# Gate groups and operand sums of a hybrid decoder layer placed ahead of, and inside, the branch products

## The chip, the cores and the metric

One core of one Trainium2 chip runs the whole layer in one launch. The metric is the device time of one execution in microseconds (us), the median of several runs. Engines are named as in the profile: PE is the matrix engine (PEld its weight loads), DVE the vector engine, ACT the scalar engine, POOL the GpSimd engine and SP the engine that issues most transfers.

## What is computed

A decoder layer on 512 tokens of width 2048, float32 in and out. The part that matters here, shortened from the reference:

```
hq, hf, hi, hg, aq, ak, av, ga, gb = split(x @ w_in)
y_a = hgrn2_mixer(hq, hf, hi, hg, ...) @ w_branch_a
y_b = swa_sink_attention(rope(aq), rope(ak), av, sinks) @ w_branch_b
mixed = sigmoid(ga) * y_a + sigmoid(gb) * y_b
x = layer_norm(ALPHA * x + mixed @ w_out, ...)
h = square(relu(x @ w_ff1)) @ w_ff2
x = layer_norm(ALPHA * x + h, ...)
```

## The kernel before

All matrix products run on PE in float32r. Each factor is split by `split` (L82) into a high half, a copy made by ACT (L84), and a low half, a subtraction made by DVE (L85). `mm3` (L113) then issues three matmuls, on L114 (high, high), L115 and L116 (one low half each). Weights arrive in blocks of 128x1024: a transfer on SP, then the two halves `wh` and `wl`.

The stages follow one another: the projections with the attention, the HGRN2 recurrence over eight heads in four pairs (`hg_pair`, L519), the branch products (L687), the gates (L712 on), the output projection with the first layer norm, and the feed-forward part.

- **Tail of the recurrence.** The last pair ends with `hg_out` (L479) once for each head: PE makes the state updates (L483), DVE chains them (L486, L488), PE makes the outputs (L493, L495), ACT squares them (L499), DVE does a dozen small steps for the root (L152 to L158) and a product (L502), PE transposes (L506), and DVE writes the head into `oT` (L508). Each step waits for the one before.
- **Branch products.** `att` (the attention's output) and `oT` (the recurrence's) are split into `half` tiles, eight slices of 128x512 each. Then eight groups of 256 columns for `wb` and eight for `wa` follow, 48 matmuls of 512 columns in a group, made by `proj_fm` (L118) with two weight blocks. ACT copies each result out of PSUM (L695), POOL stores it to `yd` (L696).
- **Gates.** `NPLAIN = 2` groups (one of gate B, one of gate A) are made the plain way, 96 matmuls of 512 columns each (`plain`, L552). The other fourteen use `Sevens` (L635), which makes seven products of half width instead of eight. It needs seven operands of the activation: four are quarters of `bh`/`bl` (one of them, q5, overwritten), three (`xq`: q3, q6, q7) are new. `operands` (L595) makes them with sums on DVE (`tt`, L590) in a scratch tile `room`, then splits them. `merge` (L701) loads `yd` into `room`, takes the sigmoid, multiplies, and stores or adds the product to `md`.

Tiles come from rings by tag: `mz` (four buffers: `att`, `oT`, later the pairs `raws` of `pair`), `h` (four: `half` tiles, `xq` tiles, `room`), `r` (two: results), `mm` (four PSUM banks). The pool of `h` and `r` lies over the memory of the recurrence, which is closed first (L541). The builder lays out one list of instructions for each engine, and each engine works its list in that order.

Of the kernel before, what the change touches and what calls it, by code (L numbers as in the profile page):

```python
# [17 lines left out]
P = 128  # L18
# [34 lines left out]
def layer(ctx, tc, xt, xn, win, wg, wa, wb, wo1, wo2, w1, w2, cst, vec, lnv, out):  # L53
# [512 lines left out]
    def flat(r):  # L566
        return r[:].rearrange("p n t -> p (n t)")
# [24 lines left out]
    def wide():  # L592
        return pf.tile([P, 4, 1024], F32, tag="h", bufs=4, name=nm("room"))

    def operands(room):  # L595

        xo = {"q1": (bh[:, 0:8, 0:CG], bl[:, 0:8, 0:CG]), "q2": (bh[:, 8:16, 0:CG], bl[:, 8:16, 0:CG]),
              "q5": (bh[:, 0:8, CG:T], bl[:, 0:8, CG:T]), "q4": (bh[:, 8:16, CG:T], bl[:, 8:16, CG:T])}
        for q in ("q6", "q7", "q3"):
            t_ = pf.tile([P, 2, 8, CG], F32R, tag="h", bufs=4, name=nm("x" + q))  # L600
            xo[q] = (t_[:, 0], t_[:, 1])
        for u in range(2):
            k = slice(4 * u, 4 * u + 4)
            r0, r1, r2, r3 = (room[:, i, :].rearrange("p (k c) -> p k c", k=4) for i in range(4))

            def whole(r, q):
                tt(r, xo[q][0][:, k, :].bitcast(F32), xo[q][1][:, k, :].bitcast(F32), ALU.add)

            def put(q, src):
                split(xo[q][0][:, k, :], xo[q][1][:, k, :], src)  # L610

            whole(r0, "q1")
            whole(r1, "q5")
            tt(r2, r0, r1, ALU.subtract)
            put("q7", r2)
            whole(r3, "q4")
            tt(r3, r1, r3, ALU.add)
            tt(r0, r3, r0, ALU.subtract)
            put("q6", r0)
            whole(r1, "q2")  # L620
            tt(r1, r1, r0, ALU.subtract)
            put("q3", r1)
            put("q5", r3)
        return xo

    def tmp(tag, bufs):
# [51 lines left out]
            self.left = (g, B, C, U2, E, t2_, b22, R)  # L678


    yd = [[pd.tile([P, 1024], F32, name=f"yd{i}_{c}") for c in range(8)] for i in range(2)]
    md = [pd.tile([P, 1024], F32, name=f"md{c}") for c in range(8)]

    def half():
        return pf.tile([P, 8, T], F32R, tag="h", bufs=4, name=nm("half"))

    for i, (w, y) in enumerate(((wb, att), (wa, oT))):  # L687
        yh, yl = half(), half()
        for k in range(8):
            split(yh[:, k, :], yl[:, k, :], y[k // 4][:, k % 4, :])  # L690
        for c in range(8):
            o = proj_fm([w[c, q] for q in range(2)], yh, yl)
            r = result()
            for m in range(2):
                ACT.activation(r[:, m, :], o[m][:], AF.Copy)  # L695
            nc.gpsimd.dma_start(out=yd[i][c][:], in_=flat(r))  # L696


    room = wide()

    def merge(g, R):  # L701

        y = room[:, 2 + g % 2, :]
        nc.scalar.dma_start(out=y, in_=yd[g % 2][g // 2][:])
        ACT.activation(R[:], R[:], AF.Sigmoid)
        tt(flat(R), flat(R), y, ALU.mult)
        if g % 2:
            nc.gpsimd.dma_start(out=md[g // 2][:], in_=flat(R), accum_op=ALU.add)
        else:
            nc.gpsimd.dma_start(out=md[g // 2][:], in_=flat(R))  # L710

    NPLAIN = 2  # L712
    for g in range(NPLAIN):
        o = [ps("mm"), ps("mm")]
        plain(wg[g], o, None)
        R = result()
        for m in range(2):
            ACT.activation(R[:, m, :], o[m][:], AF.Copy)
        if g == NPLAIN - 1:
            xo = operands(room)  # L720
        merge(g, R)
    sevens = Sevens(xo, room, merge)
    for g in range(NPLAIN, 16):
        sevens.group(g, wg[g])
# [125 lines left out]
            ACT.activation(r[:, m, :], og[g][m][:], AF.Relu)  # L850
        keep(g, r)
    room = wide()
    sevens = Sevens(operands(room), room, relu)
    for g in range(NHEAD, NG):
        sevens.group(g, w1[g])
    sevens.rest()
# [168 lines left out]
```

## Time and profile before

| | |
|---|---|
| median of 3 runs | 2714.32 us (2712.2 to 2715.52) |
| the profiled execution | 2713.84 us |
| its span on the core | 2712.1 us |
| busy: PE, DVE, ACT, POOL | 98%, 60%, 43%, 6% |
| mean granted clock of PE | 0.991 of full speed |

The span is what the trace covers; 1.74 us of the execution's time lie around it. PE's busy share counts matmuls whose ends are modelled and overlap, so 98% says that PE is nearly always at work, not how fast. The granted clock says how much of full speed (2.4 GHz) the throttle let through; 0.5 is 1.2 GHz. In rows of the timeline the columns are start, duration, engine, line, operation, output and inputs, shapes, the count, and in brackets the idle time before it and what ended that.

### The profile page before, as it was taken

Reading aid. Unit: us, or ns where it says so; the run is one execution under the profiler, and the core shown is the slowest. Engines: PE = TensorE matmul, PEld = TensorE weight load, DVE = VectorE, ACT = ScalarE, POOL = GpSimd, SP = SyncE. Lnnn points to the kernel's source line nnn. Section 1 sums busy time; section 2 is a strip of 40 time slices with the busy share of each in tenths; the row PEclk is TensorE's granted clock in tenths of the full one; section 3 lists DMA queues with packets and bytes.
Section 4 is the critical chain, followed back from the end, with each engine's and each line's share of the span. In section 5 each row is a group of like instructions: output and inputs, shape, how many; then the busy total and the mean of one; then the engine's idle time right before and its main releaser. Section 6 shows DMA issues by size and latency. Waiting matters only on the chain.

```text
span 2712.1 us, 39517 instructions
## 1 busy us (share of the span) xinstructions
PE 2652.9 (98%) x16272; PEld 2382.2 (88%) x16272; DVE 1637.7 (60%) x2121; ACT 1168.3 (43%) x1597; POOL 169.3 (6%) x168
## 2 busy tenths in 40 slices
PE   8999999998998999999999999999999999999997
PEld 7889788986887999988989999999998888888886
DVE  4588785664226878733768777777754444433346
ACT  4576655353233444421444444444444333322231
POOL 0110322210000000000200000000000000000001
PEclk9999999998998999999999999999999999999999
DMA  5222212223443455652452333333366555434442
GB/s 186 89 75 78 76 58 85 77 78 140 155 140 93 141 156 164 205 175 94 172 194 102 133 133 125 133 137 122 131 236 236 187 198 190 171 141 153 151 176 78
DMA packets 104437, 377.27 MB, mean 139 GB/s; under 512 B 11712, under 2 KB 12480, under 8 KB 102720
## 3 DMA queue, kind: packets, MB, share of 16 engines
q1 hardware_dynamic: 88128, 313.91, 33.3%
q0 software_dynamic: 10368, 41.95, 4.5%
q10 hardware_dynamic: 5760, 18.88, 2.2%
q8 instruction: 128, 2.10, 0.3%
q14 instruction: 53, 0.43, 0.0%
HBM read 332.75 MB, written 41.94 MB: 138 GB/s over the span
## 4 chain that ended last, share of the span: by engine, by line
PE 92%; DVE 5%; ACT 1%; DMA 1%; issue 1%; POOL 0%; DVEq 0%; SPq 0%; ACTq 0%
PE mm L114 21%; PE mm L116 21%; PE mm L115 21%; PE tp L116 7%; PE tp L114 7%; PE tp L115 7%; PE sc L115 1%; PE sc L114 1%; PE sc L116 1%; DVE wl L85 1%; PE tp L444 1%; DVE room L590 1%; DMA raw<-w 1%; PE tp L285 0%; PE tp L277 0%
## 5 line engine op out<-in xcount | busy, mean ns | idle before, releaser
L114 PE MATMUL mm<-bh,wh 128*128 128x256 f32 (+1 forms) x1808 | 585.6, 324 | 3.9 <-ACT wh L84 2.4
L116 PE MATMUL mm<-bh,wl 128*128 128x256 f32 (+1 forms) x1808 | 585.0, 324 | 0.5 <-DVE wl L85 0.4
L115 PE MATMUL mm<-bl,wh 128*128 128x256 f32 (+1 forms) x1808 | 585.4, 324 | 0.0
L84 ACT ACTIVATE wh<-raws 128x1024 fp32r<-128x1024 f32 x332 | 350.2, 1056 | 493.0 <-PE mm L115 319.6
L85 DVE TENSOR_TENSOR wl<-raws,wh 128x1024 fp32r<-128x1024 f32 x332 | 404.8, 1223 | 239.0 <-ACT wh L84 238.4
L85 DVE TENSOR_TENSOR wl<-raw,wh 128x1024 fp32r<-128x1024 f32 (+1 forms) x183 | 221.4, 1210 | 343.3 <-PE mm L116 193.2
L114 PEld LDWEIGHTS mm<-bh,wh 128*128 128x128 f32 x1808 | 344.9, 191 | 30.7 <-ACT wh L84 3.2
L116 PEld LDWEIGHTS mm<-bh,wl 128*128 128x128 f32 x1808 | 344.7, 191 | 26.5 <-DVE wl L85 0.9
L115 PEld LDWEIGHTS mm<-bl,wh 128*128 128x128 f32 x1808 | 344.9, 191 | 25.4
L84 ACT ACTIVATE wh<-raw 128x1024 fp32r<-128x1024 f32 (+1 forms) x183 | 190.9, 1044 | 303.9 <-PE mm L115 153.4
L85 DVE TENSOR_TENSOR hl<-raws,hh 128x1024 fp32r<-128x1024 f32 x94 | 114.8, 1224 | 235.3 <-ACT hh L84 235.1
L84 ACT ACTIVATE hh<-raws 128x1024 fp32r<-128x1024 f32 x94 | 99.1, 1058 | 264.3 <-PE mm L115 252.9
L114 PE MATMUL mm<-xq,wh 128*128 128x256 f32 x672 | 191.6, 285 | 10.8 <-ACT wh L84 10.2
L116 PE MATMUL mm<-xq,wl 128*128 128x256 f32 x672 | 191.3, 285 | 1.5 <-DVE wl L85 1.4
L115 PE MATMUL mm<-xq,wh 128*128 128x256 f32 x672 | 191.1, 284 | 0.0
L115 PE MATMUL mm<-wl,hh 128*128 128x512 f32 x472 | 183.6, 389 | 0.0
L114 PE MATMUL mm<-wh,hh 128*128 128x512 f32 x472 | 183.6, 389 | 0.0
L116 PE MATMUL mm<-wh,hl 128*128 128x512 f32 x472 | 183.6, 389 | 0.0
L114 PE MATMUL mm<-wh,bh 128*128 128x256 f32 (+1 forms) x448 | 139.2, 313 | 7.6 <-ACT bh L84 6.0
L114 PEld LDWEIGHTS mm<-xq,wh 128*128 128x128 f32 x672 | 130.1, 194 | 11.2 <-ACT wh L84 10.4
L115 PE MATMUL mm<-wl,bh 128*128 128x256 f32 (+1 forms) x448 | 138.8, 311 | 0.8 <-DVE wl L85 0.8
L114 PE MATMUL tp<-wh,hh 128*128 128x512 f32 x356 | 138.5, 389 | 0.0
(318 smaller groups left out, 5494.3 us busy)
## 6 DMA issues: line engine op xcount, KB each, us to landing
raws<-w SPq DMA_DIRECT2D x240, 512.0 KB, 4.5
raws<-hd SPq DMA_DIRECT2D x96, 512.0 KB, 3.8
raw<-win SPq DMA_DIRECT2D x87, 512.0 KB, 3.2
raws<-wg SPq DMA_DIRECT2D x56, 512.0 KB, 4.1
raw<-wo SPq DMA_DIRECT2D x32, 512.0 KB, 3.3
hd<-r POOLq DMA_DIRECT2D x32, 512.0 KB, 2.9
raw<-w SPq DMA_DIRECT2D x24, 512.0 KB, 3.6
raw<-wb SPq DMA_DIRECT2D x16, 512.0 KB, 3.6
```

The source lines that it names most:

```text
L84: ACT.activation(hi, src, AF.Copy)
L85: DVE.tensor_tensor(lo, src, hi.bitcast(F32), op=ALU.subtract)
L114: PE.matmul(o, ah, bh_, start=first, stop=False, skip_group_check=True)
L115: PE.matmul(o, ah, bl_, start=False, stop=False, skip_group_check=True)
L116: PE.matmul(o, al, bh_, start=False, stop=last, skip_group_check=True)
L444: PE.matmul(pl[:, c * P:(c + 1) * P], qk[:, c * P:(c + 1) * P], qk[:, c * P:(c + 1) * P], start=True, stop=True)
L590: DVE.tensor_tensor(dst, a, b, op=op)
```

## The change

Two plain groups of gates move ahead of the branch products, with the sigmoid in their evictions, and are stored to a new buffer `gd`. The first group of each branch (c = 0) is merged at once: `gd` is loaded into a second result tile, multiplied on DVE, and stored or added to `md`. The other seven groups of a branch go to `yd` as before. `operands` now stands after the branch products in the code, with its scratch in four `mz` pairs in place of `room`, with q7 allocated ahead of q6, and with q5 put ahead of the q2 and q3 steps. `Sevens` starts at group 2 as before. The feed-forward part calls the same `operands` with slices of `room`.

```diff
--- before.py
+++ after.py
@@ -592,16 +592,17 @@
     def wide():
         return pf.tile([P, 4, 1024], F32, tag="h", bufs=4, name=nm("room"))
 
-    def operands(room):
+    def operands(rooms):
+
 
         xo = {"q1": (bh[:, 0:8, 0:CG], bl[:, 0:8, 0:CG]), "q2": (bh[:, 8:16, 0:CG], bl[:, 8:16, 0:CG]),
               "q5": (bh[:, 0:8, CG:T], bl[:, 0:8, CG:T]), "q4": (bh[:, 8:16, CG:T], bl[:, 8:16, CG:T])}
-        for q in ("q6", "q7", "q3"):
+        for q in ("q7", "q6", "q3"):
             t_ = pf.tile([P, 2, 8, CG], F32R, tag="h", bufs=4, name=nm("x" + q))
             xo[q] = (t_[:, 0], t_[:, 1])
         for u in range(2):
             k = slice(4 * u, 4 * u + 4)
-            r0, r1, r2, r3 = (room[:, i, :].rearrange("p (k c) -> p k c", k=4) for i in range(4))
+            r0, r1, r2, r3 = (r.rearrange("p (k c) -> p k c", k=4) for r in rooms(u))
 
             def whole(r, q):
                 tt(r, xo[q][0][:, k, :].bitcast(F32), xo[q][1][:, k, :].bitcast(F32), ALU.add)
@@ -617,10 +618,10 @@
             tt(r3, r1, r3, ALU.add)
             tt(r0, r3, r0, ALU.subtract)
             put("q6", r0)
+            put("q5", r3)
             whole(r1, "q2")
             tt(r1, r1, r0, ALU.subtract)
             put("q3", r1)
-            put("q5", r3)
         return xo
 
     def tmp(tag, bufs):
@@ -678,8 +679,24 @@
             self.left = (g, B, C, U2, E, t2_, b22, R)
 
 
+    gd = [pd.tile([P, 1024], F32, name=f"gd{i}") for i in range(2)]
     yd = [[pd.tile([P, 1024], F32, name=f"yd{i}_{c}") for c in range(8)] for i in range(2)]
     md = [pd.tile([P, 1024], F32, name=f"md{c}") for c in range(8)]
+
+    def add_md(c, i, r):
+        if i:
+            nc.gpsimd.dma_start(out=md[c][:], in_=r, accum_op=ALU.add)
+        else:
+            nc.gpsimd.dma_start(out=md[c][:], in_=r)
+
+    for i in range(2):
+        o = [ps("mm"), ps("mm")]
+        plain(wg[i], o, None)
+        r = result()
+        for m in range(2):
+            ACT.activation(r[:, m, :], o[m][:], AF.Sigmoid)
+        nc.gpsimd.dma_start(out=gd[i][:], in_=flat(r))
+
 
     def half():
         return pf.tile([P, 8, T], F32R, tag="h", bufs=4, name=nm("half"))
@@ -693,9 +710,19 @@
             r = result()
             for m in range(2):
                 ACT.activation(r[:, m, :], o[m][:], AF.Copy)
-            nc.gpsimd.dma_start(out=yd[i][c][:], in_=flat(r))
-
-
+            if c:
+                nc.gpsimd.dma_start(out=yd[i][c][:], in_=flat(r))
+            else:
+                gt = result()
+                nc.sync.dma_start(out=flat(gt), in_=gd[i][:])
+                tt(flat(r), flat(r), flat(gt), ALU.mult)
+                add_md(0, i, flat(r))
+
+
+    def rooms(u):
+        return [x for _ in range(2) for x in (lambda t: (t[:, 0, :], t[:, 1, :]))(pair())]
+
+    xo = operands(rooms)
     room = wide()
 
     def merge(g, R):
@@ -704,21 +731,9 @@
         nc.scalar.dma_start(out=y, in_=yd[g % 2][g // 2][:])
         ACT.activation(R[:], R[:], AF.Sigmoid)
         tt(flat(R), flat(R), y, ALU.mult)
-        if g % 2:
-            nc.gpsimd.dma_start(out=md[g // 2][:], in_=flat(R), accum_op=ALU.add)
-        else:
-            nc.gpsimd.dma_start(out=md[g // 2][:], in_=flat(R))
+        add_md(g // 2, g % 2, flat(R))
 
     NPLAIN = 2
-    for g in range(NPLAIN):
-        o = [ps("mm"), ps("mm")]
-        plain(wg[g], o, None)
-        R = result()
-        for m in range(2):
-            ACT.activation(R[:, m, :], o[m][:], AF.Copy)
-        if g == NPLAIN - 1:
-            xo = operands(room)
-        merge(g, R)
     sevens = Sevens(xo, room, merge)
     for g in range(NPLAIN, 16):
         sevens.group(g, wg[g])
@@ -850,7 +865,7 @@
             ACT.activation(r[:, m, :], og[g][m][:], AF.Relu)
         keep(g, r)
     room = wide()
-    sevens = Sevens(operands(room), room, relu)
+    sevens = Sevens(operands(lambda u: [room[:, i, :] for i in range(4)]), room, relu)
     for g in range(NHEAD, NG):
         sevens.group(g, w1[g])
     sevens.rest()
```

How the lists of instructions move, at three places. First PE, from the last projection of the recurrence (`mm_5588`) into the two `hg_out` of the last pair; before:

```order
L116 MATMUL mm_5588<-wh_5752,bl 128x256
L483 MATMUL sc_5808<-v_5805,kT_5461 128x128 x3
L493 MATMUL sc_5816<-v_5805,SB_2016 128x128 x2
L495 MATMUL sc_5816<-state_5812,qe_5450 128x128
L493 MATMUL sc_5816<-v_5805,SB_2016 128x128
L495 MATMUL sc_5816<-state_5812,qe_5450 128x128
L493 MATMUL sc_5816<-v_5805,SB_2016 128x128
L495 MATMUL sc_5816<-state_5812,qe_5450 128x128
L506 MATMUL sc_5847<-ident,on_5825 128x128 x4
L483 MATMUL sc_5853<-v_5805,kT_5585 128x128 x3
```

Now the matmuls of the plain groups (`mm_5929` is the first PSUM bank of the first one) stand around these steps:

```order
L116 MATMUL mm_5929<-bh,wl_5933 128x512
L114 MATMUL mm_5929<-bh,wh_5932 128x512
L483 MATMUL sc_5808<-v_5805,kT_5461 128x128 x3
L115 MATMUL mm_5929<-bl,wh_5932 128x512
L116 MATMUL mm_5929<-bh,wl_5933 128x512
```

Of the 192 plain matmuls, 19 now stand ahead of the first L483, 25 between it and L493, 45 from there to L506, 23 to the second L483, 25 to L493, 46 to the second L506, and nine after it; then the first branch group begins. Before, none stood between these steps.

Second, ACT where the branch products begin; before:

```order
L499 ACTIVATE on_5825,ss_5824<-sc_5816 128x128 x4
L499 ACTIVATE on_5870,ss_5869<-sc_5861 128x128 x4
L84 ACTIVATE half_5927<-att_522 128x512 x4
L84 ACTIVATE half_5927<-att_523 128x512 x4
L84 ACTIVATE half_6473<-oT_2020 128x512 x4
```

and now:

```order
L499 ACTIVATE on_5870,ss_5869<-sc_5861 128x128 x4
L84 ACTIVATE wh_6202<-raw_6201 128x1024
L84 ACTIVATE wh_6232<-raw_6231 128x1024
L697 ACT_TABLE_LOAD
L697 ACTIVATE r_6051<-mm_5929 128x512
L697 ACTIVATE r_6051<-mm_5930 128x512
L697 ACTIVATE r_6177<-mm_6055 128x512
L84 ACTIVATE half_6181<-att_522 128x512 x4
L84 ACTIVATE half_6181<-att_523 128x512 x4
```

The evictions of the plain groups (L697, with a table load) now stand between the last squares of the recurrence and the first `half`. On DVE in the same stretch the sums of `operands` (L590 on `raws`) now stand between the halves and the `wl` of the first four branch groups:

```order
L590 TENSOR_TENSOR raws_7282<-bh,bl 128x1024 x2
L85 TENSOR_TENSOR half_6182<-att_523,half_6181 128x512
L85 TENSOR_TENSOR half_6731<-oT_2020,half_6730 128x512 x3
L85 TENSOR_TENSOR wl_6272<-raw_6270,wh_6271 128x1024
L85 TENSOR_TENSOR half_6731<-oT_2020,half_6730 128x512
L85 TENSOR_TENSOR half_6731<-oT_2021,half_6730 128x512 x2
L590 TENSOR_TENSOR raws_7283<-raws_7282 128x1024
L590 TENSOR_TENSOR raws_7283<-bh,bl 128x1024
L85 TENSOR_TENSOR half_6731<-oT_2021,half_6730 128x512 x2
L590 TENSOR_TENSOR raws_7300<-bh,bl 128x1024 x2
L85 TENSOR_TENSOR wl_6302<-raw_6300,wh_6301 128x1024
L590 TENSOR_TENSOR r_6261<-r_6261,r_6264 128x1024
```

`wl_6272` and `wl_6302` belong to the second branch group, and row L590 on `r_6261` is the product of the first merged group. In the list of before this stretch has the 16 halves and then nothing but `wl`.

Third, ACT where `Sevens` begins, behind the last branch product (`mm_7213`, `mm_7214`; `wh_7363` is the first split out of `room`):

```order
L712 ACTIVATE r_7275<-mm_7213 128x512
L84 ACTIVATE xq_1123_7281<-raws_7282 128x1024
L84 ACTIVATE xq_1123_7281<-raws_7300 128x1024
L712 ACTIVATE r_7275<-mm_7214 128x512
L731 DMA room_7318<-yd_1_5906 128x1024
L731 DMA room_7318<-yd_1_5914 128x1024
L84 ACTIVATE wh_7363<-room_7318 128x1024
L84 ACTIVATE wh_7392<-raws_7326 128x1024
```

Before, at the same place, ACT's list had the evictions, sigmoids and operand splits of the plain groups:

```order
L718 ACTIVATE r_7271<-mm_7149 128x512
L718 ACTIVATE r_7271<-mm_7150 128x512
L705 ACTIVATE r_7271<-r_7271 128x1024
L84 ACTIVATE xq_1121_7275<-room_7019 128x1024
L660 ACTIVATE E_7317<-mm_7313 128x256
L84 ACTIVATE bh<-room_7019 128x4x256
L84 ACTIVATE xq_1120_7274<-room_7019 128x1024
L704 DMA room_7019<-yd_1_5904 128x1024
L704 DMA room_7019<-yd_0_5911 128x1024
L84 ACTIVATE xq_1122_7276<-room_7019 128x1024
L84 ACTIVATE wh_7357<-room_7019 128x1024
```

Only the splits of q3 (`xq_1123`) are left there; those of q7, q6 and q5 moved up into the branch products. But for a few rows in the first two groups of `Sevens`, all lists are the same as before from there on.

## Rows read from the trace of the kernel before

**Rows 1.** The page, busy time, share of the span, instructions of each engine
```profile
PE 2652.9 (98%) x16272; PEld 2382.2 (88%) x16272; DVE 1637.7 (60%) x2121; ACT 1168.3 (43%) x1597; POOL 169.3 (6%) x168
```

**Rows 2.** Waits of PE, whole span: who waited for whom, us, times, longest
```profile
PE mm L114 <- ACT wh L84: 14.2, 6, 10.2
PE sc L506 <- DVE on L502: 8.9, 2, 4.4
```

**Rows 3.** Windows: stretch, length, busy PE PEld DVE ACT POOL, PEclk, DMA share, GB/s
```profile
612.26:641.26 29.00, 16.18 (x63) 13.01 (x64) 16.09 (x48) 10.54 (x31) 0.00 (x0) 0.65 0.14 49
858.74:876.70 17.96, 6.17 (x26) 5.59 (x26) 17.10 (x15) 7.38 (x9) 0.90 (x1) 0.62 0.51 127
641.26:855.84 214.58, 214.58 (x949) 177.77 (x948) 70.10 (x63) 65.72 (x83) 9.32 (x17) 1.00 0.43 146
```

**Rows 4.** Timeline of the recurrence's tail, ACT and PE
```profile
616.03 0.39 PE L495 MATMUL sc<-state,qe 128*128 128x128 f32 x2
...
620.85 1.09 PE L506 MATMUL sc<-ident,on 128*128 128x128 f32 x4 [4.43 <-DVE on L502]
...
634.54 4.27 ACT L84 ACTIVATE half<-att 128x512 fp32r<-128x512 f32 x8 [4.43 <-PE sc L506]
```

**Rows 5.** Timeline of an earlier head, matmuls of the same kind at full clock
```profile
348.39 0.39 PE L495 MATMUL sc<-state,qe 128*128 128x128 f32 x2
348.61 0.39 PE L493 MATMUL sc<-v,SB 128*128 128x128 f32 x2
```

**Rows 6.** Timeline of PE where `Sevens` starts
```profile
858.34 0.28 PE L115 MATMUL mm<-bl,wh 128*128 128x256 f32 x1
858.46 0.28 PE L116 MATMUL mm<-bh,wl 128*128 128x256 f32 x1
868.98 0.58 PE L114 MATMUL mm<-xq,wh 128*128 128x256 f32 x1 [10.24 <-ACT wh L84]
...
872.12 0.58 PE L116 MATMUL mm<-xq,wl 128*128 128x256 f32 x1 [1.40 <-DVE wl L85]
```

**Rows 7.** Tile `half` and line L705: count, duration ns min/median/max, first and last start
```profile
L84 ACT ACTIVATE half<-att x8: 610/612/629, 634.5 to 638.2; 128x512 fp32r<-128x512 f32 x8
L85 DVE TENSOR_TENSOR half<-att,half x8: 684/685/691, 635.2 to 639.4; 128x512 fp32r<-128x512 f32 x8
...
L705 ACT ACTIVATE r<-r x16: 1042/1044/1062, 836.8 to 1160.8; 128x1024 f32<-128x1024 f32 x16
L705 ACT ACT_TABLE_LOAD  x1: 1283/1283/1283, 835.5 to 835.5; - x1
```

**Rows 8.** Timeline of DVE and ACT around the operands: steps of 128x1024 operations
```profile
846.05 1.22 DVE L85 TENSOR_TENSOR xq<-room,xq 128x1024 fp32r<-128x1024 f32 x1
847.19 1.22 DVE L85 TENSOR_TENSOR bl<-room,bh 128x1024 fp32r<-128x1024 f32 x1
...
863.20 1.46 ACTq L704 DMA_DIRECT2D room<-yd  x2
...
868.83 1.99 ACT L84 ACTIVATE wh<-raws 128x1024 fp32r<-128x1024 f32 x2
```

**Rows 9.** Short idle times of PE elsewhere, and windows of 2 us behind the second
```profile
347.84 0.71 PE L493 MATMUL sc<-v,SB 128*128 128x128 f32 x4 [1.71 <-DVE state L488]
1345.82 0.63 PE L792 MATMUL tp<-ident,z 128*128 128x128 f32 x4 [1.33 <-DVE z L783]
...
1347.00:1349.00 2.00, 1.58 (x9) 1.47 (x8) 2.00 (x3) 2.00 (x4) 0.60 (x2) 0.66 0.30 59
1349.00:1351.00 2.00, 2.00 (x11) 2.00 (x11) 2.00 (x4) 2.00 (x4) 2.00 (x2) 0.50 0.98 350
```

**Rows 10.** Tiles `yd`, `md`, `room`, in order: transfers from issue to landing, min/median/max
```profile
DMA to landing us min/median/max: 2.9/4.7/7.2
DMA to landing us min/median/max: 2.9/5.4/9.4
DMA to landing us min/median/max: 3.3/4.0/6.1
```

## Prediction

> **What bounds the kernel now.** The page comes first: PE is busy for 98% of the span and no other engine for more than 60% [rows 1]. So time is saved only where PE idles or runs at half clock. The second view, the waits of PE, says where: the longest single wait is 10.2 us for ACT's weight halves, and DVE's product `on` (L502) costs 8.9 us in two pieces [rows 2]. The third view, windows over the stretches around these waits, gives their price with the clock in it [rows 3]. In the first, 612.26 to 641.26 us, the granted clock is 0.65; in the second, 858.74 to 876.70, it is 0.62. Between them lie 214.58 us with 949 matmuls of 512 columns, at full clock and without a gap: 0.226 us for one.
>
> *First gap, the tail of the recurrence.* The window has 63 matmul rows. Fifteen are of the first branch group: 15 x 0.226 = 3.4 us. The other 48 belong to the last two heads. At full clock two such rows start 0.22 us apart [rows 5], 0.11 for one, so they are 5.3 us of work. Of 29.0 us, 20.3 are lost. The timeline shows how: PE ends L495 at about 616.4, and idles 4.43 us until DVE delivers `on` at 620.85; from there it runs at half clock [rows 4].
>
> *Second gap, the start of `Sevens`.* The window has 26 matmuls of 256 columns, which start 0.12 us apart at full clock [rows 6]: 3.1 us of work in 17.96, so 14.8 lost. PE waits 10.24 us for ACT's split of `room` and 1.40 more for DVE's [rows 6], while DVE works without a pause (17.10 of 17.96 us, [rows 3]) on the operand sums, which could not be finished beside the two plain groups.
>
> Together 35.1 us are lost. PE's work is the same before and after, so the forecast is these 35.1 us less what the new order loses in its own places.
>
> **The change, part by part.** *Plain groups into the tail.* 192 matmuls x 0.226 = 43.4 us of PE work now stand between the steps of the two heads. By the list, 45 of them (10.2 us) separate L495 from the first L506, and 46 the second. The chain that they cover took 4.8 us (616.03 to 620.85, [rows 4]); two `wl` halves that DVE now makes ahead of it add 2 x 1.14 us (the step of such operations, [rows 8]), and one of them waits up to 0.9 us for the end of a weight block. That is 8.0 us against 10.2. The shorter steps have 23 to 25 matmuls, over 5 us, for under 3 us of DVE work. Nothing here should be waited for: 20.3 us come back, and the first branch group starts at full clock.
>
> *Start of the branch products.* `half` lies over memory of the recurrence, so ACT begins only when the second L506 has ended, as before [rows 4]. New in front of it are a table load and three evictions. The load is 1.28 us [rows 7]; an eviction has the shape of a `half` copy, which start 0.6 us apart or less [rows 7]. With the first copy: 1.28 + 3 x 0.6 + 0.61 = 3.7 us. The transposes end some 0.25 us after PE goes on, and the nine plain matmuls behind them cover 2.0. PE waits 3.7 + 0.25 - 2.0 = 2.0 us. The low half then takes DVE 0.69 us [rows 7], of which two matmuls cover 0.45: 0.3 more. Cost 2.3 us. The trace has sixteen sigmoids with copies among them and one load [rows 7], after which the next operation starts at once; so one load is charged and no second one for the copies behind. The Trainium skill ("ScalarE: Activation LUTs", What ACT_TABLE_LOAD costs) speaks against this place: it puts a drain of about 1.38 us beside the 1.28 us of each switch. By an estimate from that page the wait here would be 3.7 us and not 2.3, and the sum 1.4 us worse.
>
> *Operand sums into the branch products.* The sums, 16 operations, and six of the eight low halves of 128x1024 leave the second gap; the two of q3 stay at the start of `Sevens`. By the list most of the sums stand on DVE among the halves and `wl` of the first four branch groups. From the first low half to the second `wl` of branch group two, DVE has 16 halves x 0.6, six sums and two `wl` x 1.14: 18.7 us. PE passes 78 matmuls, 17.6 us, from 0.75 us later: it waits 0.4. To the next `wl` DVE has four operations (4.6 us) against 20 matmuls (4.5), then six (6.8) against 28 (6.3), then two against 20. In all 0.9 us, and nothing after that. On ACT six splits, about 1 us each [rows 8], lie beside PE, since ACT is at 31% there (65.72 of 214.58, [rows 3]).
>
> *The merged first groups.* These replace two merges of the gates, one for one: the same sigmoid, product and store. What is new is the detour: a gate goes to `gd` and back, two transfers. The gate's product on DVE stands ahead of a `wl`, and the second of two result tiles holds the gate, so ACT's eviction of the next group waits for it. The walk from the last plain eviction, some 5.4 us after the first `half` copy began: store 4.7 and load 4.0 us, the medians of such transfers [rows 10], puts the gate in its tile about 15 us after that copy. DVE reaches the product at about 19, ACT needs the tile at about 23. With the worst landings, 9.4 and 6.1 [rows 10], the gate is there at 22 and DVE loses 3. I take 0, and keep 3 for the range. The load sits on SP ahead of the weights of branch group four, needed only 10 us later.
>
> *Start of `Sevens`.* The scratch `room` is free when the last branch product ends. PE has 24 matmuls, 2.9 us, that do not need it. ACT has two splits of q3, an eviction and two transfers to issue ahead of the split of `room`: 2 x 1.0 + 0.6 + 1.46 + 1.05 = 5.1 us [rows 8]. PE waits 2.2, makes two matmuls, waits for the next split, 1.0 less 0.25: 3.0 in all. Then there is the clock. An idle time of 1.71 us at 346 left it alone; one of 1.33 with a second short one, at 1345, was followed by half clock for about 3.4 us [rows 9], which costs 1.5 (16 matmuls at twice 0.12, less rounding). The two waits here look like the second case: 1.5 charged. At the start of the branch products I charge none, since a slow PE there would use up the 0.9 us that it waits for DVE anyway; the upper bound is another 1.5.
>
> *Elsewhere.* The feed-forward part calls the same function, but its lists stay in the same order: nothing. The transfers are the same but for two stores and two loads of 512 KB.
>
> **Sum.** 35.1 - (2.3 + 0.9 + 3.0 + 1.5) = 27.4 us. From the profiled execution's 2713.84 that gives 2686.4; the median of the runs shown is 0.48 us higher, so 2687. With no fall of the clock and no wait for DVE it would be 2684; with the clock falling twice and the gate late, 2691. So the likeliest case spans 2682 to 2691.
>
> **Rivals.** *The branch start stays a gap.* At its old start PE took 6.8 us from the end of L506 (634.46) for 3.4 us of work [rows 3, 4], with ACT and DVE splitting just ahead of it at half clock. If that stays and the 3.1 us of load and evictions come on top, the place loses 6.5 us and not 2.3; with the clock and the gate at their bounds this gives 2691 to 2698. For it: ACT and DVE are still one slice ahead. Against it: PE now arrives at full clock, and one slice (six matmuls, 1.36 us) outlasts a step of ACT or DVE (0.6).
>
> *The gate comes late, and the kernel gets slower.* DVE's list is in order, so a gate that lands late stops the product, the `wl` behind it and with them PE, and ACT behind the result tile as well. It happens twice. To use up 27.4 us and 5.4 more, each gate would have to hold up PE for over 16 us, so a store and load of some 26 us, where the slowest seen are 9.4 and 6.1 [rows 10]. If each took 30 us, the time would be about 2727. Only a store stuck behind others on POOL's queue could do that, and POOL is at 6% [rows 1].
>
> *It does not do what it says*: if DVE's steps stood too close to PE's in the new tail, PE would wait for `on` as before and the plain groups would cover little; with the sums gone from the second gap only, 2703, and with new waits in the branch products near 2713. The list, with 45 and 46 matmuls ahead of L506, speaks against it.
>
> **How the numbers follow.** Both gaps filled, 2682 to 2691: 0.74. Better still, below 2682: 0.03. A gap left at the branch start, 2691 to 2698: 0.16. One gap unfilled, 2698 to 2708: 0.02. No change: 0.03. Slower by the gate: 0.02. A measurement tells about 0.2%, 5.4 us, from no change. So faster 0.95, same 0.03, slower 0.02. The range 2680 to 2697 leaves out about one case in eight.
>
> **What would show it.** In the changed profile PE's wait for `on` (8.9 us) and the one of 10.2 us for ACT are gone from the waits; the steps L483 to L506 of the last pair stand among matmuls at a granted clock of 1.00. A wait of 2 to 2.5 us on ACT's `half` ends the plain groups some 48.5 us after the last projection; waits on DVE's `wl` of under 1 us follow in the first 35 us; at the start of `Sevens` one of about 2.2 us on ACT and one under 1 us. The sums show on DVE between the first branch groups. I am wrong if a wait of over 5 us appears on `half`, on the gate's tile, or on a raw weight block behind its load, or if the clock drops to half in the tail.

## The result, and the profile after

| | before | after |
|---|---|---|
| median of 4 runs | 2714.02 us (2712.2 to 2715.52) | 2682.27 us (2681.08 to 2683.24) |
| the profiled execution | 2713.84 us | 2682.10 us |
| mean granted clock of PE | 0.991 | 0.997 |

The ratio is 0.9883 (95% interval 0.9866 to 0.9900): 31.75 us less. The forecast was 2687, range 2680 to 2697. So the sign and the places were right, the gain was 4.4 us larger than its sum of 27.4, and the time lies at the lower edge of the likeliest case, 2682 to 2691. On the page PE is at 99% of a shorter span, with nearly the same work as in [rows 1]:

```profile
PE 2642.8 (99%) x16272; PEld 2373.6 (89%) x16272; DVE 1637.1 (61%) x2121; ACT 1164.7 (43%) x1595; POOL 169.2 (6%) x168
```

To compare kernels without the noise of the feed-forward part, I measure one stretch in each. It begins with the last matmul of L468, near the end of the last projection of the recurrence. It has two ends: the last matmul of the gates, which gives the *PE stretch*, and the sigmoid of the last merge, which the expectations below use. The first and the last row of the PE stretch, before and after, then the view of the sigmoids of the merges after, L732 (count, duration in ns, first and last start); for those of before see L705 in [rows 7]:

```profile
610.68 0.39 PE L468 MATMUL tp<-prl,ones 128*128 128x512 f32 x1
...
1154.05 0.28 PE L116 MATMUL tp<-xq,wl 128*128 128x256 f32 x1
```

```profile
610.92 0.39 PE L468 MATMUL tp<-prl,ones 128*128 128x512 f32 x1
...
1123.33 0.28 PE L116 MATMUL tp<-xq,wl 128*128 128x256 f32 x1
```

```profile
L732 ACT ACTIVATE r<-r x14: 1042/1044/1044, 867.1 to 1128.9; 128x1024 f32<-128x1024 f32 x14
```

To the sigmoid the stretch is 1160.8 - 610.7 = 550.1 us before and 1128.9 - 610.9 = 518.0 after, 32.1 us less. On PE it is 543.37 and 512.41, 31.0 us less. The two differ because the sigmoid is an operation of ACT that comes 6.7 us (before) and 5.6 us (after) behind PE's last matmul of the gates, when PE is at work on the output projection. So PE's own saving is 31.0 us. What is left of PE's waits in it, from 600 to 900 us (who waited for whom, us, times, longest), in place of the 10.2 and 8.9 us of [rows 2]:

```profile
PE mm L114 <- issue: 1.5, 1, 1.5
PE mm L114 <- ACT wh L84: 0.5, 1, 0.5
PE tp L114 <- ACT wh L84: 0.4, 1, 0.4
PE mm L116 <- DVE wl L85: 0.2, 1, 0.2
```

Windows over the same places (stretch, length, busy PE PEld DVE ACT POOL, PEclk, DMA share, GB/s), which answer to [rows 3]:

```profile
612.26:660.90 48.64, 48.64 (x241) 40.96 (x240) 18.54 (x44) 12.61 (x27) 0.00 (x0) 1.00 0.26 87
660.90:666.00 5.10, 3.61 (x16) 2.39 (x15) 4.19 (x6) 5.09 (x11) 0.78 (x1) 1.00 0.42 91
666.00:839.00 173.00, 172.70 (x763) 142.41 (x762) 74.37 (x70) 59.33 (x80) 8.90 (x16) 1.00 0.46 153
839.00:850.00 11.00, 10.05 (x80) 9.54 (x80) 10.97 (x11) 7.13 (x9) 0.53 (x1) 1.00 0.93 336
```

The first is the new tail: 48.64 us long, PE busy for all of it, at clock 1.00. The others are the branch start (5.10 - 3.61 = 1.49 us idle), the branch products (0.30 idle) and the start of `Sevens` (0.95 idle). No window has a lower clock.

Idle time is less than what PE loses. It is counted from the modelled end of a matmul (0.39 us for one of 512 columns, where the next starts after 0.226), and it leaves out the slower steps right behind a wait. The prediction priced its gaps by steps, from the start of one matmul to the start of the next, 0.226 us at full pace for 512 columns and 0.12 for 256. Counted the same way, from the rows below, the branch start loses 2.0 us, the two waits for `wl` in the branch products 0.8, the start of `Sevens` 1.6. Together 4.5 us are lost, where the sum charged 7.7.

**Branch start.** ACT, DVE and PE, by start:

```profile
659.62 1.28 ACT L697 ACT_TABLE_LOAD   x1 [3.03 <-PE sc L506]
660.91 1.57 ACT L697 ACTIVATE r<-mm 128x512 f32<-128x512 f32 x3
662.36 4.28 ACT L84 ACTIVATE half<-att 128x512 fp32r<-128x512 f32 x8
```

```profile
661.70 1.23 DVE L85 TENSOR_TENSOR wl<-raw,wh 128x1024 fp32r<-128x1024 f32 x1 [1.36 <-PE mm L116]
663.04 1.29 DVE L85 TENSOR_TENSOR half<-att,half 128x512 fp32r<-128x512 f32 x2
```

```profile
661.22 0.39 PE L116 MATMUL mm<-bh,wl 128*128 128x512 f32 x1
663.10 0.70 PE L114 MATMUL mm<-half,wh 128*128 128x512 f32 x2 [1.49 <-issue]
663.78 0.50 PE L115 MATMUL mm<-half,wh 128*128 128x512 f32 x1
664.12 0.39 PE L116 MATMUL mm<-half,wl 128*128 128x512 f32 x1
```

ACT's chain is the one forecast: the load begins when L506 ends, the eviction 1.29 us later, the first `half` at 662.36. But three evictions take 1.45 us and not 1.8. DVE is hardly behind: its `wl` for the second weight block begins when the last plain matmul has released the buffer (661.70), and the low half follows it. PE goes on at 663.10. The first matmul with the low half (L115) comes 0.68 us later, where two steps take 0.45, so the low half holds PE up by some 0.2 us that the view doesn't show as idle. From 661.22 to 664.12 PE makes four steps in 2.90 us, 0.90 at full pace: 2.0 lost. The view's name for the wait, "issue", says that PE waited for nothing that the profile shows.

**Branch products.** Two matmuls wait for a `wl`, at 681.90 and here:

```profile
693.25 0.73 PE L116 MATMUL mm<-half,wl 128*128 128x512 f32 x2 [0.15 <-DVE wl L85]
```

The matmul ahead of this row starts at 692.72, the one behind its two at 693.82: three steps in 1.10 us, 0.68 at full pace. That is 0.4 lost, and as much at 681.90.

**Start of `Sevens`.** ACT and its DMA queue, then PE:

```profile
838.52 1.05 ACT L84 ACTIVATE xq<-raws 128x1024 fp32r<-128x1024 f32 x1
838.67 0.82 ACTq L731 DMA_DIRECT2D room<-yd  x2
839.47 1.05 ACT L84 ACTIVATE xq<-raws 128x1024 fp32r<-128x1024 f32 x1
840.42 0.59 ACT L712 ACTIVATE r<-mm 128x512 f32<-128x512 f32 x1
840.90 1.05 ACT L84 ACTIVATE wh<-room 128x1024 fp32r<-128x1024 f32 x1
```

```profile
841.21 0.28 PE L116 MATMUL mm<-bh,wl 128*128 128x256 f32 x1
842.00 0.39 PE L114 MATMUL mm<-xq,wh 128*128 128x256 f32 x1 [0.51 <-ACT wh L84]
...
842.95 0.39 PE L114 MATMUL tp<-bh,wh 128*128 128x256 f32 x1 [0.44 <-ACT wh L84]
...
843.69 0.28 PE L115 MATMUL mm<-xq,wh 128*128 128x256 f32 x1
```

The two transfers are issued at 838.67, in the middle of ACT's work, although the list has them behind the second eviction, which began at 840.42. So the order of the list held for ACT's operations and not for these issues. The split of `room` ends at 841.95, some 3.5 us after the last branch product, not 5.1. From 841.21 to 843.69 PE makes seven steps in 2.48 us, 0.84 at full pace: 1.6 lost, of which 0.67 stand ahead of 842.00.

**The second gate.** DVE's product for branch a, and SP's wait ahead of the load of the gate:

```profile
770.18 1.23 DVE L590 TENSOR_TENSOR r<-r,r 128x1024 f32<-128x1024 f32 x1 [6.40 <-DMA r<-gd]
```

```profile
SPq L717 <- DMA yd<-r: 5.1, 1, 5.1
```

Here the gate came late: DVE stood 6.40 us. PE waited for nothing there.

### The profile page after: what moved, and what is told of

The parts are those of the page before. It is cut to its first block, busy times and chain, and to the rows that moved or that the text cites. A ratio compares the mean times of both kernels' runs of the same rounds, so it can differ in the third digit from the quotient of the medians.

```text
span 2680.3 us, 39522 instructions
## 1 busy us (share of the span) xinstructions
PE 2642.8 (99%) x16272; PEld 2373.6 (89%) x16272; DVE 1637.1 (61%) x2121; ACT 1164.7 (43%) x1595; POOL 169.2 (6%) x168
## 4 chain that ended last, share of the span: by engine, by line
PE 92%; DVE 4%; issue 2%; ACT 1%; DMA 1%; POOL 0%; DVEq 0%; SPq 0%; ACTq 0%; POOLq 0%
PE mm L116 21%; PE mm L114 21%; PE mm L115 21%; PE tp L114 7%; PE tp L115 7%; PE tp L116 7%; PE sc L114 1%; PE sc L116 1%; PE sc L115 1%; DVE wl L85 1%; PE tp L444 1%; PE tp L285 0%; DMA raw<-win 0%; PE tp L277 0%; DMA raw<-w 0%
## 5 line engine op out<-in xcount | busy, mean ns | idle before, releaser
L115 PE MATMUL mm<-bl,wh 128*128 128x256 f32 (+1 forms) x1808 | 585.3, 324 | 0.0
L115 PEld LDWEIGHTS mm<-bl,wh 128*128 128x128 f32 x1808 | 344.5, 191 | 25.3
L115 PE MATMUL mm<-xq,wh 128*128 128x256 f32 x672 | 190.3, 283 | 0.0
L115 PE MATMUL mm<-wl,hh 128*128 128x512 f32 x472 | 183.7, 389 | 0.0
L115 PE MATMUL mm<-wl,bh 128*128 128x256 f32 (+1 forms) x448 | 139.0, 311 | 0.8 <-DVE wl L85 0.8
L116 PE MATMUL tp<-wh,hl 128*128 128x512 f32 x356 | 138.6, 389 | 0.0
```

The costliest lines, as they stand in the source:

```text
L115: PE.matmul(o, ah, bl_, start=False, stop=False, skip_group_check=True)
L116: PE.matmul(o, al, bh_, start=False, stop=last, skip_group_check=True)
```

## Experiments

All kernels below are timed against the kernel before in the same batch. Its medians there were 2711.33 (first four), 2713.04 (next four), 2712.64 (`again`, `warm_sev`, `warm_pool_sev`) and 2712.86 (`pool_wl`).

| run | median, us | ratio to before, 95% interval | stretch to the sigmoid, us | PE stretch, us |
|---|---|---|---|---|
| the changed kernel | 2682.27 | 0.9883 (0.9866 to 0.9900) | 518.0 | 512.41 |
| `tail_only` | 2696.82 | 0.9946 (0.9931 to 0.9960) | 533.3 | 527.01 |
| `ops_only` | 2698.93 | 0.9952 (0.9937 to 0.9967) | 536.0 | 529.61 |
| `one_ahead` | 2692.63 | 0.9932 (0.9916 to 0.9949) | 529.3 | 524.07 |
| `long_wait` | 2688.01 | 0.9913 (0.9898 to 0.9927) | 523.2 | 518.30 |
| `warm` | 2683.20 | 0.9892 (0.9878 to 0.9907) | 517.2 | 512.17 |
| `gate_raw` | 2686.12 | 0.9901 (0.9886 to 0.9915) | 523.2 | 516.63 |
| `best` | 2684.11 | 0.9894 (0.9880 to 0.9909) | 521.6 | 515.14 |
| `issue_sp` | 2682.19 | 0.9886 (0.9869 to 0.9902) | 517.5 | 512.40 |
| `again` | 2682.80 | 0.9887 (0.9872 to 0.9902) | 517.2 | 512.38 |
| `warm_sev` | 2682.19 | 0.9886 (0.9871 to 0.9901) | 516.6 | 511.56 |
| `warm_pool_sev` | 2681.19 | 0.9881 (0.9865 to 0.9898) | 518.0 | 511.64 |
| `pool_wl` | 2681.33 | 0.9885 (0.9868 to 0.9901) | 517.3 | 512.86 |

`again` is the changed kernel once more:

> The changed kernel once more, so that the two below stand beside it on the same chip: 2682 us.

To the sigmoid its stretch differs by 0.8 us from the first one, so less than 1 us in that column tells nothing. The PE stretches of these two and of `issue_sp`, which has the same waits, lie within 0.03 us, so there a difference of some tenths counts, though each rests on one profiled execution.

### The two halves of the change

`tail_only`:

```diff
-        for q in ("q7", "q6", "q3"):
+        for q in ("q6", "q7", "q3"):
...
-    xo = operands(rooms)
     room = wide()
+    xo = operands(lambda u: [room[:, i, :] for i in range(4)])
```

> Only the first half of the change: the plain groups stay ahead of the branch products, the operand sums stand behind the branch products again, in `room`. Theory (two gaps, two covers): the tail of the recurrence stays filled, no wait of PE for `on`; but the plain groups that stood beside the sums are gone from there. By the list DVE has some 13 operations of 1.14 us, 15 us, between the last branch product and the low half that `Sevens` needs first, against 2.9 us of PE work: PE waits 10 to 12 us there, and with a fall of the clock some 15 us are lost, as in the second gap of before. 2697 us (2693 to 2702). Rival (filling the tail brings nearly all, the sums find room beside the last branch products anyway): 2682 to 2686.

`ops_only`, against the kernel before:

```diff
-    def operands(room):
+    def operands(rooms, late=None):
...
-            put("q5", r3)
+            if late is None:
+                put("q5", r3)
...
+    late = []
+    xo = operands(rooms, late)
     room = wide()
...
         if g == NPLAIN - 1:
-            xo = operands(room)
+            for hi, lo, s in late:
+                split(hi, lo, s)
```

(`late` keeps q5's sums until the plain groups have read what they overwrite.)

> Only the second half: the sums in the mixers' tiles during the second branch, the plain groups behind the branch products as before, and the split of q5 kept until they are done, since they read what it overwrites. Theory: the second gap (14.8 us lost) shrinks to 1 us or less, the tail keeps its 20.3 us and its two waits of 4.4 us for `on`: 2714.0 - 14 = 2700 us (2698 to 2702). Rival (the sums hold up the low halves and `wl` of the first branch group, where PE stands at half clock behind the tail): 4 to 8 us of new waits there, 2703 to 2708.

Both first theories held. In `tail_only` the tail is filled and one wait stands at the start of `Sevens`, longer than the 10.24 us of [rows 6]:

```profile
855.25 0.58 PE L114 MATMUL mm<-xq,wh 128*128 128x256 f32 x1 [14.68 <-ACT wh L84]
```

In `ops_only` that wait is gone, and the two for `on` are those of [rows 2] (waits of PE, 600 to 920 us):

```profile
PE sc L506 <- DVE on L502: 8.9, 2, 4.4
...
PE mm L116 <- DVE wl L85: 0.5, 1, 0.5
```

On PE the halves save 16.4 and 13.8 us, 30.1 together, and the whole change 31.0. So each gap has its own cover; but the plain groups had covered sums at their old place, and when they move alone, the wait behind grows from 10.24 to 14.68 us.

### How much cover the tail needs

`one_ahead`:

```diff
+    gate(0)
...
     for i, (w, y) in enumerate(((wb, att), (wa, oT))):
+        if i:
+            gate(1)
```

(`gate(i)` is the body of the loop over the plain groups.)

> One plain group ahead of the branch products instead of two; the other stands between the two branches. By the list it fills the steps of the last but one head and leaves 7 matmuls among those of the last head. Theory (each step needs matmuls of its own between itself and the next): one wait of about 4.4 us for `on` is back, and half clock behind it: half of the 20.3 us of the tail, 2692 us (2689 to 2696). Rival (the price of the tail was the clock, and one filled head keeps it up): 2 to 4 us more than with both ahead, 2684 to 2686.

2692.63 against 2692: the last head, left with 7 matmuls, waits as before, and behind it stands the branch start at half clock:

```profile
645.38 0.92 PE L506 MATMUL sc<-ident,on 128*128 128x128 f32 x4 [4.43 <-DVE on L502]
649.37 2.05 PE L114 MATMUL mm<-half,wh 128*128 128x512 f32 x4 [3.07 <-ACT half L84]
```

The PE stretch is 11.7 us longer than in the changed kernel. Each step needs matmuls of its own; the cover of one head does not carry over to the next.

### The branch start: two chains

`warm`, in `hg_out`:

```diff
+        if hh == HG_HEADS - 1:
+            ACT.activation(warm[:], on[:, T - 1:T], AF.Sigmoid)
```

> One sigmoid of a single column directly behind the last squares, so that the table load stands there, in ACT's idle time; the lists of all engines are otherwise those of the changed kernel. Theory (the load is 1.28 us of the chain that ends PE's wait at the branch start): ACT's first eviction starts at once when the last L506 ends, the wait of 1.49 us falls to about 0.2, and the time to 2681.0 us. Rival (a switch costs more than its row, or the wait then hangs on the low half): the wait stays at 0.6 to 1 us, 2681.7 us.

The load moved away, and PE's wait hardly shrank. ACT, DVE and PE:

```profile
649.41 0.22 ACT L499 ACTIVATION_READ_ACCUMULATOR on<-sc 128x1 f32 x1
649.64 1.28 ACT L501 ACT_TABLE_LOAD   x1
650.94 0.20 ACT L501 ACTIVATE warm<-on 128x1 f32<-128x1 f32 x1
```

```profile
661.50 1.22 DVE L85 TENSOR_TENSOR wl<-raw,wh 128x1024 fp32r<-128x1024 f32 x1 [1.36 <-ACT half L84]
662.64 4.29 DVE L85 TENSOR_TENSOR half<-att,half 128x512 fp32r<-128x512 f32 x7
```

```profile
661.57 0.70 PE L114 MATMUL mm<-half,wh 128*128 128x512 f32 x2 [0.17 <-issue]
663.38 0.51 PE L115 MATMUL mm<-half,wh 128*128 128x512 f32 x1 [1.10 <-DVE half L85]
```

PE starts the branch at 661.57 after 0.17 us, makes two matmuls and waits 1.10 for the low half: 1.27 instead of 1.49. DVE's `wl` could begin only at 661.50, when the last plain matmul was done, and the low half stands behind it. (The row names ACT's `half`; but this `wl` begins 0.48 to 0.49 us after the last plain matmul in both kernels, at 661.22 and 661.01.) Two chains ended almost together, and the prediction had priced one. On PE 0.24 us are gained. On the load: it begins at 649.64, where the last square's read-out ends, and the next operation at 650.94, where the load ends.

`gate_raw` goes further:

```diff
-        r = result()
+        r = pw.tile([P, 1024], F32, tag="raw", bufs=3, name=nm("gate"))
```

> The plain groups are evicted into tiles of the `raw` ring, which does not lie over the memory of the recurrence, in place of `r`. Load and evictions then come as soon as a group is finished. Theory (the wait at the branch start is load plus three evictions, 2.8 us, ahead of the first `half`): it goes entirely, 2680.8 us. Rival (a gate holds one of three `raw` buffers until its store has landed, some 5 us, and a weight load comes late): waits of 1 to 3 us for ACT's `wh` in the tail, 2682 to 2684 us.

It lost 3.9 us (4.2 on PE) against `issue_sp`, which ran in the same batch with the changed kernel's order of work. ACT's first `half` now comes before PE is done with the plain groups, but with other ready times the builder laid out another order: in DVE's list five low halves and two sums more stand ahead of the next `wl`, 5 x 0.6 + 2 x 1.14 = 5.3 us. PE, then windows:

```profile
662.01 0.50 PE L115 MATMUL mm<-half,wh 128*128 128x512 f32 x1 [1.52 <-DVE half L85]
...
676.72 0.73 PE L116 MATMUL mm<-half,wl 128*128 128x512 f32 x2 [1.78 <-DVE wl L85]
```

```profile
661.00:666.00 5.00, 3.99 (x17) 3.30 (x18) 5.00 (x9) 5.00 (x11) 0.54 (x1) 1.00 0.55 210
...
676.00:681.00 5.00, 4.28 (x12) 3.42 (x13) 5.00 (x5) 1.06 (x1) 0.00 (x0) 0.68 0.29 105
```

A wait of 1.52 us for the low half, then one of 1.78 for that `wl`, and a clock of 0.68 behind it. The rival that I had named, weights late behind a held buffer, explains at most a later wait of 0.97 us for `wh`; the order on DVE is what I hold for the main loss, though no run changed it alone.

`best` moves the product with q5 ahead of the one with q6 in the first group of `Sevens`, on top of `gate_raw`:

```diff
+            if self.n == 0:
+                prod1(C, xo["q5"], b11, True, False)
             t2_ = self.room[:, self.n % 2, :]
```

> As the one with the `raw` ring, and in the first group of `Sevens` the product with q5 ahead of the one with q6, which needs `room`: 48 matmuls of 256 columns instead of 24 cover ACT's splits at its start (5.8 us for the 3.5 that ACT needs from the last branch product). Theory: the waits of 0.51 and 0.44 us there go as well: 2680 us (2679 to 2681). Rival (the wait moves to the sum or split that q5's weights need): 2680.8 us, as without this part.

PE's two waits at the start of `Sevens` are gone, and the PE stretch is 1.5 us shorter than that of `gate_raw`. As it carries the loss of `gate_raw`, the total missed. So this move was put on `warm` instead:

> The changed kernel with the early table load and, in the first group of `Sevens`, the product with q5 ahead of the one with q6. Theory: the wait at the branch start stays at 1.3 us, on DVE's `wl` and low half, as with the early load alone; the two waits at the start of `Sevens` (0.95 us) go: 1 to 1.7 us less than the changed kernel from the last projection of the recurrence to the last sigmoid of the merges (518.0 us there in its trace), 2681 us in all. Rival: the waits move to the sum or the split that q5's weights need, 0 to 0.3 us less.

The same 1.10 us for the low half, and 0.8 in two waits for `wl`, one of 0.62 at 851.83 new. The waits at the start of `Sevens` are gone. On PE 0.85 us are gained, 0.24 of them as in `warm`, less than the 1 to 1.7 expected; the medians don't show it. Then POOL was to take DVE's part, first the low half, then the `wl` (in whose expectation "a quarter less" should read "half of that"):

```diff
+            if i == 0 and k < 1:
+                ACT.activation(yh[:, k, :], src, AF.Copy)
+                POOL.tensor_tensor(yl[:, k, :], src, yh[:, k, :].bitcast(F32), op=ALU.subtract)
```

> As the one before, and POOL makes the first low half, which DVE makes behind a `wl` that waits for the last plain matmul. Theory (two chains end at the branch start almost together, ACT's with the load and DVE's with that `wl`): with both shortened the wait falls from 1.3 to about 0.6 us, since POOL takes some 1.3 us for such an operation where DVE takes 0.69: 0.6 us less than the one before. Rival (POOL's operation is slower there, or waits behind its DMA issue): the wait stays at 1.3 us or grows.

```diff
-            split(wh[:], wl[:], raw[:])
+            ACT.activation(wh[:], raw[:], AF.Copy)
+            (low or DVE).tensor_tensor(wl[:], raw[:], wh[:].bitcast(F32), op=ALU.subtract)
```

> As the one with the early table load and the moved q5 product, and POOL makes the one `wl` that stands ahead of the first low half on DVE (128x1024, for the second weight block of the first branch group); PE needs it 5.4 us later. POOL took 1.99 us for a quarter less than that, 128x512, beside DVE, so some 4 us here. Theory (DVE's list, that `wl` behind the last plain matmul and then the low half, is the second chain that ends at the branch start): the wait of 1.1 us for the low half goes, 515.6 us from the last projection to the last sigmoid instead of 516.6, and 2680.5 to 2681.5 us in all. Rival (POOL and DVE slow each other, or POOL's `wl` comes late): a wait of 1 to 3 us for it some 5 us behind the branch start.

Neither rid PE of the wait: 1.63 us for POOL's low half in the first, 2.58 for DVE's in the second, with PE stretches 0.1 and 1.3 us longer than that of `warm_sev`. In `pool_wl`, the tile `half`, POOL, and PE's wait:

```profile
L85 DVE TENSOR_TENSOR half<-att,half x8: 678/680/3299, 659.6 to 668.7; 128x512 fp32r<-128x512 f32 x8
```

```profile
659.99 2.38 POOL L94 TENSOR_TENSOR wl<-raw,wh 128x1024 fp32r<-128x1024 f32 x1
```

```profile
662.99 0.50 PE L116 MATMUL mm<-half,wh 128*128 128x512 f32 x1 [2.58 <-DVE half L85]
```

One of DVE's eight low halves took 3.30 us instead of 0.68 while POOL worked 2.38: DVE's result came only when POOL was done. In `warm_pool_sev` it was POOL's turn: 1.99 us beside DVE's `wl`, where its products of 128x512 in the recurrence (L462) take 1.29. The Trainium skill ("SBUF — State Buffer", SBUF: two separate sides) has this as a lock: an operation of DVE with two inputs in SBUF and one of POOL that reads SBUF exclude each other for the whole instruction, and the one that starts first goes first. Both traces agree with the exclusion, 3.30 us and 1.99; the order in `pool_wl` does not, since by the rows DVE's operation began 0.36 us before POOL's and still came last.

By the medians no version beats the changed kernel by more than the scatter: the two lowest lie 1.5 and 1.6 us under `again`. On PE the shortest stretches are 0.85 and 0.77 us shorter, those of `warm_sev` and `warm_pool_sev`.

### The clock behind a wait

`long_wait`, an operation more on ACT that the halves overwrite:

```diff
+        if i == 0:
+            ACT.activation(yh[:, :, 0:CG], bh[:, 0:8, 0:CG].bitcast(F32), AF.Copy)
```

> A copy of 128x2048 on ACT ahead of the first `half`, whose result the halves overwrite: about 2 us, so PE's wait at the branch start grows from 1.49 us to some 3.5. The order of a few of the following matmuls and low halves changes with it. Theory A (the prediction's charge for the clock): behind a wait of this length the granted clock falls to half for some 3.4 us, which costs 1.5 us beside the 2: 2685.5 us. Theory B (one wait between long stretches at full work leaves the clock alone): clock 1.00 behind it and 2684.3 us. The window behind the wait tells them apart better than the time.

The builder also put a weight split and an eviction ahead of the halves, so the wait grew to 4.72 us (PE, then windows):

```profile
666.11 2.05 PE L114 MATMUL mm<-half,wh 128*128 128x512 f32 x4 [4.72 <-issue]
```

```profile
668.00:670.00 2.00, 2.00 (x6) 1.61 (x5) 2.00 (x3) 2.00 (x5) 0.00 (x0) 0.50 0.39 156
...
672.00:674.00 2.00, 2.00 (x11) 1.62 (x10) 2.00 (x5) 1.79 (x4) 0.00 (x0) 1.00 0.70 254
```

The clock was at 0.50 behind it and back at 672. Of the 5.9 us by which the PE stretch is longer, 3.2 are the longer wait. From 666.11 to 671.71 thirteen steps take 5.60 us, where full pace takes 2.9, which is 2.3 more than the same place loses in the changed kernel. The rest, 0.4, is a wait of 0.95 us for a `wh` at 681.68 in place of the two for `wl`. Theory A held for this length in kind; the price was 2.3 us and not 1.5.

A shorter wait is on record too: `pool_wl` shows a fall of the clock behind its 2.58 us (windows):

```profile
663.00:666.00 3.00, 3.00 (x10) 2.40 (x11) 3.00 (x5) 3.00 (x6) 0.58 (x1) 0.72 0.52 180
666.00:670.00 4.00, 4.00 (x16) 3.18 (x15) 4.00 (x7) 3.05 (x7) 0.00 (x0) 0.78 0.33 131
```

From 664.61 to 667.59 seven steps take 2.98 us there, 0.43 each, which is half clock; full pace takes 1.6, so these steps alone cost 1.4. For 3.5 us nothing was measured.

### Transfers issued by ACT

`issue_sp`:

```diff
-        nc.scalar.dma_start(out=y, in_=yd[g % 2][g // 2][:])
+        nc.sync.dma_start(out=y, in_=yd[g % 2][g // 2][:])
```

> The loads of `yd` in the merges are issued by SP in place of ACT, nothing else. The prediction charged 1.46 us for two of them on ACT ahead of the split of `room`. Theory A (the charge was wrong: the issues run beside ACT's operations, as the trace of the changed kernel has them at 838.67, in the middle of an eviction and a split): the splits start when they did, 0.5 us of waiting for `room` stays, 2682.3 us. Theory B (they cost their time on ACT): that wait goes, and each later merge gives ACT 0.3 us, which PE does not wait for: 2681.6 us.

Theory A: the waits at the start of `Sevens` are the same 0.5 and 0.4 us, the PE stretch (512.40 and 512.41) and the time too. Issuing costs ACT nothing there.

## Why the prediction was right, and where its sum was off

- *Tail of the recurrence* (20.3 us back, nothing lost): right. The tail has no wait and a full clock; `tail_only` and `one_ahead` show that it is the matmuls between the steps that do it.
- *Operand sums* (14.8 us back): right, shown by `ops_only` against the kernel before and by `tail_only` against the changed one. Of the 0.9 us charged for waits of PE on `wl`, 0.8 came.
- *Branch start* (2.3): 2.0 by steps, of which 1.49 show as idle time. The evictions were charged at 0.6 us each and stepped at 0.48; of the 0.3 for the low half some 0.2 came. So the size was nearly right. One step failed all the same: the chain was priced on ACT alone. `warm` shows a second chain, the last plain matmul, `wl`, low half, 0.2 us behind it, so that the load's 1.28 us, which the sum counted in full, are worth only 0.2. That the second chain ended just ahead of the first, and left the size as it was, is luck. A second price for the table load, which would have made the wait 3.7 us, is not in the trace: the load of the changed kernel and that of `warm` are followed at once by the next operation. The Trainium skill's figure for a drain ("ScalarE: Activation LUTs", What ACT_TABLE_LOAD costs) is shown by neither.
- *Start of `Sevens`* (3.0): 1.6 by steps. The mis-sized term is the 1.46 us for issuing two transfers. It was read off a row of ACT's queue at a time when ACT stood idle; with work in front of it ACT issues beside it. Without this term the wait of 2.2 would have been 0.7, and 0.67 was lost there.
- *Clock* (1.5): nothing, 1.00 in every window. I set two waits of 2.2 and 0.75 us beside those of 1345 us in [rows 9]; the real ones were 0.51 and 0.44. That was not a wrong price but waits that never became as long; where a wait did, the 2.58 us of `pool_wl`, the half clock cost at least 1.4.
- *Merged first groups* (0, with 3 for the range): PE lost nothing, but the walk was right for one branch only. It found the gate early by DVE's pace in branch b, where 16 halves and six sums stand ahead of the product. In branch a nothing does, and SP's load waited 5.1 us for the result tile that the last group of branch b was still being stored from. DVE stood 6.40 us. This is the rival's mechanism, at a price that PE did not see.
- *Rivals*: a gap left at the branch start of 6.5 us did not appear; in `one_ahead`, where PE comes to it from a wait, 3.07 us of waiting for `half` are back. The other two did not occur.

The errors, 0.3 + 0.1 + 1.4 + 1.5 = 3.3 us, all went one way; 35.1 - 4.5 = 30.6 us against 31.0 on PE. The other 0.8 us of the 31.75 in the medians lie outside the PE stretch, where the work is the same; among the changed kernel, `again` and `issue_sp` the part behind it alone differs by up to 1.2 us, so they are scatter as far as can be told.

## What to carry to other kernels

Where PE waits in a chain of short steps, independent matmuls between the steps bring back more than the wait, since PE then keeps its clock; but count them for each step, and ask what they had covered at their old place. Before shortening the chain that ends a wait, look which chain ends next: here the second was 0.2 us behind, and of four attempts to gain 1.3 us there the best gained 0.2. In a program whose lists are laid out by a builder, one early ready time can reorder another engine and cost more than it saves. To tell such small gains, measure between two rows of the engine that bounds the kernel: the PE stretches of one order of work lay within 0.03 us, those to an operation of ACT within 0.8.

## What the runs showed of the hardware

- Two transfers in ACT's list were issued at 838.67, ahead of an eviction that stands before them in the list and began at 840.42; moving them to SP changed nothing.
- A subtraction of DVE and one of POOL did not run together: 3.30 us instead of 0.68 for the one, 1.99 instead of 1.29 for the other.
- Waits of PE and the clock behind them: 1.49 us (changed kernel) and 1.52 (`gate_raw`) were followed by 1.00, 1.78 (`gate_raw`) by 0.68 in a window of 5 us, 2.58 (`pool_wl`) by 0.72 in one of 3 us, 4.72 (`long_wait`) by 0.50. What tells the second and third apart is left open.
